# Hybrid decoder layer on one core: pieces of the third output column block placed between the seven products of the output projection

## The chip, the cores and the metric

The kernel runs on one core of one Trainium2 chip. The time is device microseconds (us) of one launch. Before the change it is 789.38 us, the median of 3 runs (789.31 to 791.33). A profiled execution of the same kernel took 789.26 us; its trace spans 787.5 us.

## The reference, cut to what matters

One layer on an input `x` of 256 tokens by 2048 channels, in float32. Two token mixers (gated DeltaNet and block attention) give `oa` and `ob`, each 256 x 1024. What follows them is the part that the change touches:

```
u_a = oa @ w_branch_a          # (256,1024) @ (1024,2048)
u_b = ob @ w_branch_b
merged = sigmoid(gate_a) * u_a + sigmoid(gate_b) * u_b
y = merged @ w_out             # (256,2048) @ (2048,2048)
out = x + rms_norm(y, post_norm_w)
```

## The kernel before, in words

**How a product is made.** TensorE works on float32 numbers that are split in two: `split` (L220 to L225) has ScalarE copy a raw piece of weights to a shorter format (`hi`, L223), and then VectorE subtract that from the raw piece (`lo`, L224). Three matmuls stand for one: hi by hi, hi by lo, lo by hi. One load of weights is 512 rows by 512 columns, 1 MB, issued by SyncE into one of three `raw` buffers. It is split in two **pieces**, each of 128 x 1024 numbers (two steps of 128 rows). `hi` and `lo` have three buffers each, so that piece n can be split only when TensorE has done with piece n-3. In the usual form (`proj_n`) a piece feeds two PSUM banks, one for each half of the tokens: 12 matmuls, a *double* piece. A piece that feeds one bank has 6 matmuls, a *single* piece.

**The order of the end of the kernel.** For each of four column blocks `c` of 512 channels the main loop makes `u_a` (`proj_n` with `wa`, four double pieces), multiplies the gate `ga` by it (L955), makes `u_b` (`wb`, four double pieces), multiplies `gb` (L958), and adds the two (L959). `merge(c)` then transposes the sum (`mt`, 2 x 4 matmuls of 128 x 128 on TensorE) and splits it into `mT` (ScalarE L929, VectorE L930).

The output projection has four column blocks as well. The top half of the first two column blocks (rows 0 to 1023 of `w_out`, columns 0 to 1023) is made by Strassen's scheme with **seven products** in place of eight: `product(...)` calls named yp1, yp5, yp6, yp2, yp7, yp3, yp4, each of two single pieces. They need sums of quarters of `mT` (four sums, made in `merge(1)` on VectorE, L935 to L938, and split by ScalarE L941 and VectorE L942) and differences of quarters of `w_out` (`tq`, six halves made by `differences()`, L915, and two more at L1003). The quarter `tq[0]` can be loaded, by GpSimd's queue (L903), only when the last sum is split, since it takes the sums' memory. Then come the bottom halves of column blocks 0 and 1 (double pieces, y0 and y1), then the whole of column block 2 (`proj_n` "y2", eight double pieces), then column block 3 (y3): its pieces are all split first (`keep`, L1058 and L1059, and two through `split`), and then multiplied for the first half of the tokens and for the second, each followed by its normalisation and output.

**What sets the order around the change.** Small jobs are Python generators in queues (`mq` for merges, `sq` for differences); `tick()` is called after every two-bank step of 128 rows (6 matmuls), in `product` after every one-bank step too, and lets a job go on when the units that it yielded have run out (half a unit per tick). So `yield 2` means four ticks. A list scheduler then lays out each engine's instructions; TensorE's order is the program's. ScalarE, VectorE and the DMA queues each work strictly through their own list. PSUM has eight banks: four for `acc` (here the four Strassen results c21, c11, c12, c22), four for `aux` (transposes).

Of the kernel before, what the change touches and what calls it, by code (L numbers as in the profile page):

```python
# [12 lines left out]
ALU = mybir.AluOpType  # L13
# [58 lines left out]
def hybrid_layer(  # L72
# [15 lines left out]
    nc = tc.nc  # L88
    B, S, D = x.shape
    NT = S // P  # L90
    KT = D // P
# [10 lines left out]
    wo = w_out.rearrange("o d f -> (o d) f")  # L102
# [16 lines left out]
    def acc_tile(name):  # L119
        return acc.tile([P, 512], F32, tag="acc", name=name)  # L120

    def aux_tile(name):
        return aux.tile([P, 512], F32, tag="aux", name=name)

    gq, vq, mq = Queue(), Queue(), Queue()
# [6 lines left out]
    def tick():  # L132
        after[0] -= 0.5
        for q in (gq, vq, mq, *aq, *extra):
            q.tick()
# [3 lines left out]
    def mm(*args, **kwargs):  # L139
        return pin(nc.tensor.matmul(*args, **kwargs))  # L140
# [79 lines left out]
    def split(raw, shape, name):  # L220
        hi = wspl.tile(shape, F32R, tag="hi", name=f"hi_{name}")
        lo = wspl.tile(shape, F32R, tag="lo", name=f"lo_{name}")
        nc.scalar.copy(hi, raw)  # L223
        nc.vector.tensor_tensor(lo, raw, hi.bitcast(F32), op=ALU.subtract)  # L224
        return hi, lo  # L225
# [9 lines left out]
    def turn(c):  # L235

        ks = range(CHUNKS[c], CHUNKS[c + 1])
        each = 1 if len(ks) == 2 else 2
        pts = []
        for i, k in enumerate(ks):  # L240
            if i % each == 0:
                pt = aux_tile(f"hTp_{k}")
            pts.append(pt[:, (i % each) * S : (i % each + 1) * S])
            for t in range(NT):
                tr(pts[-1][:, t * P : (t + 1) * P], xs[t][:, k * P : (k + 1) * P], ident)
        return [(k, pts[i]) for i, k in enumerate(ks)]
# [44 lines left out]
    pts = turn(0)  # L291
# [7 lines left out]
    for c in range(NCH):  # L299
        first_products("k", c, *sk_)  # L300
        if c == 0:
            pts = turn(1)
# [7 lines left out]
        if c + 2 < NCH:  # L310
            pts = turn(c + 2)
# [50 lines left out]
    def proj_n(w, col, stat, nk, name):  # L362

        pts = [acc_tile(f"a_{name}_{t}") for t in range(NT)]
        for kb in range(nk // 4):
            raw = wraw.tile([P, 4, 512], F32, tag="raw", name=f"raw_{name}_{kb}")
            nc.sync.dma_start(raw, w[kb * 512 : (kb + 1) * 512, col : col + 512].rearrange("(k p) c -> p k c", p=P))
            for u in range(2):
                hi, lo = split(raw[:, 2 * u : 2 * u + 2, :], [P, 2, 512], f"{name}_{kb}_{u}")
                for kk in range(2):  # L370
                    k = kb * 4 + u * 2 + kk
                    for t in range(NT):
                        sh = stat[:, k, t * P : (t + 1) * P]
                        sl = stat[:, k, S + t * P : S + (t + 1) * P]
                        mm(pts[t], sh, hi[:, kk, :], start=(k == 0), stop=False)
                        mm(pts[t], sh, lo[:, kk, :], start=False, stop=False)
                        mm(pts[t], sl, hi[:, kk, :], start=False, stop=(k == nk - 1))
                    tick()
        return pts
# [180 lines left out]
    def lazily(make):  # L560
        made = []

        def get():
            if not made:
                made.append(make())
            return made[0]

        return get
# [117 lines left out]
    ga = big.tile([P, D // 512, NT, 512], F32, tag="ga", name="ga")  # L686

    def free_tile(shape, dtype, tag, name):
        gq.drain()
        return big.tile(shape, dtype, tag=tag, name=name)  # L690

    gb_tile = lazily(lambda: free_tile([P, D // 512, NT, 512], F32, "g1", "gb"))
# [172 lines left out]
    for blk in ORDER:  # L865
        n, c = blk[:2].rstrip("0123456789"), int(blk[-1])
# [17 lines left out]
    mT = big.tile([P, KT, 2 * S], F32R, tag="hT", name="mT")  # L884
# [23 lines left out]
    load_quarter(2, 0, 0)  # L908

    def differences():  # L910
        yield 4
        for o, a, b in ((0, 0, 2), (1, 1, 0), (2, 1, 2)):
            for u in range(2):
                us = slice(2 * u, 2 * u + 2)
                nc.vector.tensor_tensor(tq[o][:, us], tq[a][:, us], tq[b][:, us], op=ALU.subtract)  # L915
                yield 2

    def merge(c):
        yield 1
        p3s = []  # L920
        for t in range(NT):
            pt = aux_tile(f"mt_{c}_{t}")
            for q in range(4):
                tr(pt[:, q * P : (q + 1) * P], ga[:, c, t, q * P : (q + 1) * P], ident)
            p3 = pt.rearrange("p (k n) -> p k n", n=P)
            p3s.append(p3)
            hi = mT[:, 4 * c : 4 * c + 4, t * P : (t + 1) * P]
            lo = mT[:, 4 * c : 4 * c + 4, S + t * P : S + (t + 1) * P]
            nc.scalar.copy(hi, p3)  # L929
            nc.vector.tensor_tensor(lo, p3, hi.bitcast(F32), op=ALU.subtract)  # L930
            if c == 0:
                nc.scalar.copy(sf[:, t], p3)
            yield 0.5
        if c == 1:
            nc.vector.tensor_tensor(sf[:, 2], p3s[1], sf[:, 1], op=ALU.add)  # L935
            nc.vector.tensor_tensor(sf[:, 3], sf[:, 2], sf[:, 0], op=ALU.subtract)
            nc.vector.tensor_tensor(sf[:, 1], sf[:, 0], sf[:, 1], op=ALU.subtract)
            nc.vector.tensor_tensor(sf[:, 0], p3s[0], sf[:, 3], op=ALU.subtract)  # L938
            yield 0.5
            for i, j in enumerate((2, 3, 1, 0)):  # L940
                nc.scalar.copy(SH[i], sf[:, j])  # L941
                nc.vector.tensor_tensor(SL[i], sf[:, j], SH[i].bitcast(F32), op=ALU.subtract)  # L942
                yield 0.5
            load_quarter(0, 0, 1)
            formed.append(True)
            sq.add(differences())
# [5 lines left out]
    for c in range(D // 512):  # L952
        pa = proj_n(wa, c * 512, oaT[0], H, f"ua{c}")
        for t in range(NT):
            nc.vector.tensor_tensor(ga[:, c, t, :], ga[:, c, t, :], pa[t], op=ALU.mult)  # L955
        pb = proj_n(wb, c * 512, ob_tile(), H, f"ub{c}")
        for t in range(NT):
            nc.vector.tensor_tensor(gb_tile()[:, c, t, :], gb_tile()[:, c, t, :], pb[t], op=ALU.mult)  # L958
            nc.vector.tensor_tensor(ga[:, c, t, :], ga[:, c, t, :], gb_tile()[:, c, t, :], op=ALU.add)  # L959
        mq.add(merge(c))  # L960


    sq.drain()
# [3 lines left out]
    def quarter(t, h):  # L967

        ks = slice(4 * h, 4 * h + 4)
        return mT[:, ks, t * P : (t + 1) * P], mT[:, ks, S + t * P : S + (t + 1) * P]  # L970

    def load(h, c):
        raw = wraw.tile([P, 4, 512], F32, tag="raw", name=f"raw_y{c}_{h}")
        nc.sync.dma_start(raw, wo[h * 512 : (h + 1) * 512, c * 512 : (c + 1) * 512].rearrange("(k p) c -> p k c", p=P))
        return raw

    def product(a, raw, banks, first, name):

        for u in range(2):
            hi, lo = split(raw[:, 2 * u : 2 * u + 2, :], [P, 2, 512], f"{name}_{u}")  # L980
            for kk in range(2):
                k = 2 * u + kk
                for (ah, al), pt, new in zip(a, banks, first):
                    mm(pt, ah[:, k], hi[:, kk, :], start=(new and k == 0), stop=False, skip_group_check=True)
                    mm(pt, ah[:, k], lo[:, kk, :], start=False, stop=False, skip_group_check=True)
                    mm(pt, al[:, k], hi[:, kk, :], start=False, stop=(k == 3), skip_group_check=True)
                tick()
# [2 lines left out]
    kept = big.tile([P, 3, 512], F32, tag="u1", name="kept")  # L990
    s1, s5, v = (kept[:, i] for i in range(3))
    s_ = list(zip(SH, SL))
    product([quarter(0, 0)], load(0, 0), [c21], [True], "yp1")
    product([s_[0]], tq[0], [c12], [True], "yp5")
    nc.scalar.copy(s1, c21)
    raw21 = load(1, 0)
    product([s_[1]], tq[1], [c21], [False], "yp6")
    nc.scalar.copy(s5, c12)
    product([quarter(0, 1)], raw21, [c11], [True], "yp2")
    nc.vector.tensor_tensor(c12, c21, s5, op=ALU.add)  # L1000
    for u in range(2):
        us = slice(2 * u, 2 * u + 2)
        nc.vector.tensor_tensor(tq[1][:, us], raw21[:, us], tq[1][:, us], op=ALU.subtract)  # L1003
    product([s_[2]], tq[2], [c21], [False], "yp7")
    product([s_[3]], load(1, 1), [c12], [False], "yp3")
    nc.vector.tensor_tensor(v, c21, s5, op=ALU.add)
    product([quarter(1, 1)], tq[1], [c21], [False], "yp4")

    postw = big.tile([P, D], F32, tag="z2", name="postw")
# [29 lines left out]
    for c, banks, late in ((0, (c11, c21), (c11, s1)), (1, (c12, c22), (c22, v))):  # L1039
# [2 lines left out]
        nc.vector.tensor_tensor(late[0], late[0], late[1], op=ALU.add)  # L1042
        for t in range(NT):
            weigh(c, t, banks[t])
    pts = proj_n(wo, 2 * 512, mT, KT, "y2")

    c, pts2 = 3, pts
    pts = [acc_tile(f"a_y{c}_{t}") for t in range(NT)]
    keep = [big.tile([P, 2, 2, 2, 512], F32R, tag=tg, name=f"keep_{tg}") for tg in ("g0", "ga", "u1")]
    parts = []  # L1050
# [51 lines left out]
```

## Time and profile before

| what | value |
|---|---|
| median of 3 runs | 789.38 us |
| profiled execution | 789.26 us |
| its span in the trace | 787.5 us |
| TensorE matmul busy | 98% of the span |
| VectorE busy | 67% |
| ScalarE busy | 52% |
| granted TensorE clock, mean | 0.998 |

The profile's page gives busy time by engine, 40 slices of the span, the chain of work that ended last, and the costliest groups of instructions. The trace behind it can be asked for one stretch: the busy time of each engine there, the instructions in order of time with what ended the idle time before them, and who waited for whom. Matmuls overlap each other by the profile's account (one of 128 x 512 is shown as 0.39 us long, while the next starts 0.23 us after it), so TensorE's starts say more than its ends.

### The profile page before, as it was taken

The page shows a single profiled execution, that of the slowest core. Times are in us where ns is not written, and L with a number is a line of the kernel's source. Part 1 is how long each engine was busy: PE and PEld are TensorE (multiplying, and loading weights), DVE is VectorE, ACT ScalarE, POOL GpSimd, SP SyncE. Part 2 cuts the span into 40 slices and gives each one's busy share as a digit, 9 for nine tenths or more (in the row PEclk, how much of TensorE's full clock was granted, in tenths as well). Part 3 has the DMA queues.
Part 4 walks back from the last instruction along what each step waited for, and adds up shares of the span by engine and source line. Part 5 has one row for each costly group of instructions (what it writes and reads, how often), then busy time and mean ns, then how long its engine had stood idle before and what let it go on. Part 6 is the DMA issues. An engine that isn't in the chain of part 4 may idle for free.

```text
span 787.5 us, 10153 instructions
## 1 busy us (share of the span) xinstructions
PE 771.8 (98%) x3869; PEld 647.6 (82%) x3869; DVE 531.5 (67%) x875; ACT 413.3 (52%) x624; POOL 26.2 (3%) x53
## 2 busy tenths in 40 slices
PE   8999999999999999999999999999999999999995
PEld 6878888888888888888888988888888887878884
DVE  5877885885868898864446556555545669797563
ACT  5776655554644545455365646454554444465451
POOL 3010000100100000020000000000000000000000
PEclk9999999999999999999999999999999999999999
DMA  9857656655596555686336375555466646667542
GB/s 269 263 148 221 202 165 177 210 162 164 175 277 226 188 191 189 209 221 207 107 108 199 124 219 178 187 163 164 158 214 213 203 172 213 195 228 260 174 159 107
DMA packets 95249, 149.78 MB, mean 190 GB/s; under 512 B 5152, under 2 KB 47184, under 8 KB 94560
## 3 DMA queue, kind: packets, MB, share of 16 engines
q1 hardware_dynamic: 92000, 136.46, 54.5%
q0 software_dynamic: 2624, 11.63, 5.1%
q10 hardware_dynamic: 576, 1.05, 0.4%
q8 instruction: 30, 0.49, 0.3%
q14 instruction: 19, 0.16, 0.1%
HBM read 145.95 MB, written 3.17 MB: 189 GB/s over the span
## 4 chain that ended last, share of the span: by engine, by line
PE 94%; DVE 2%; SPq 1%; ACT 1%; DMA 1%; issue 1%; DVEq 0%; ACTq 0%
PE a_ga L140 11%; PE a_gb L140 11%; PE a_y L140 10%; PE a_mk L140 6%; PE a_v L140 6%; PE a_mq L140 6%; PE a_zg L140 6%; PE a_zm L140 6%; PE a_ua L140 5%; PE a_q L140 5%; PE a_k L140 5%; PE a_ub L140 5%; PE a_mv L140 5%; PE sv L140 2%; PE s L140 1%; DMA x<-in_x_dram 1%
## 5 line engine op out<-in xcount | busy, mean ns | idle before, releaser
L140 PE MATMUL a_ga<-hi_ga,hT 128*128 128x512 f32 x256 | 82.2, 394 | 0.0
L140 PE MATMUL a_gb<-hi_gb,hT 128*128 128x512 f32 x256 | 82.1, 394 | 0.0
L224 DVE TENSOR_TENSOR lo_gb<-raw_gb,hi_gb 128x1024 fp32r<-128x1024 f32 x32 | 39.2, 1224 | 41.1 <-ACT hi_gb L223 41.1
L224 DVE TENSOR_TENSOR lo_ga<-raw_ga,hi_ga 128x1024 fp32r<-128x1024 f32 x32 | 39.0, 1223 | 30.2 <-ACT hi_ga L223 30.1
L223 ACT CAST hi_gb<-raw_gb 128x1024 fp32r<-128x1024 f32 x32 | 33.7, 1052 | 48.5 <-PE a_gb L140 34.5
L223 ACT CAST hi_ga<-raw_ga 128x1024 fp32r<-128x1024 f32 x32 | 33.5, 1051 | 47.1 <-PE a_ga L140 30.3
L140 PEld LDWEIGHTS a_ga<-hi_ga,hT 128*128 128x128 f32 x256 | 48.1, 188 | 11.0 <-issue 1.0
L140 PEld LDWEIGHTS a_gb<-hi_gb,hT 128*128 128x128 f32 x256 | 48.1, 188 | 10.0
L140 PE MATMUL a_ga<-lo_ga,hT 128*128 128x512 f32 x128 | 50.1, 391 | 0.0
L140 PE MATMUL a_gb<-lo_gb,hT 128*128 128x512 f32 x128 | 49.8, 389 | 0.0
L140 PE MATMUL a_k<-hT,hi_k 128*128 128x512 f32 x128 | 46.5, 404 | 0.1
L140 PE MATMUL a_mk<-hT,hi_mk 128*128 128x512 f32 x128 | 46.1, 401 | 0.0
L140 PE MATMUL a_mq<-hT,hi_mq 128*128 128x512 f32 x128 | 45.7, 400 | 0.0
L140 PE MATMUL a_q<-hT,hi_q 128*128 128x512 f32 x128 | 45.6, 397 | 0.0
L140 PE MATMUL a_v<-hT,hi_v 128*128 128x512 f32 x128 | 45.3, 397 | 0.0
L140 PE MATMUL a_y<-hi_y,mT 128*128 128x512 f32 x144 | 44.8, 389 | 0.0
L140 PE MATMUL a_ua<-hi_ua,oaT 128*128 128x512 f32 x128 | 41.8, 395 | 0.0
L140 PE MATMUL a_zg<-hi_zg,hT 128*128 128x512 f32 x128 | 40.6, 391 | 0.0
L140 PE MATMUL a_zm<-hi_zm,hT 128*128 128x512 f32 x128 | 40.5, 392 | 0.0
L140 PE MATMUL a_mv<-hi_mv,hT 128*128 128x512 f32 x128 | 40.5, 392 | 0.0
L140 PE MATMUL a_ub<-hi_ub,obT 128*128 128x512 f32 x128 | 40.1, 389 | 0.0
L140 PE MATMUL a_k<-hT,lo_k 128*128 128x256 f32 x128 | 36.2, 283 | 0.0
(333 smaller groups left out, 1906.1 us busy)
## 6 DMA issues: line engine op xcount, KB each, us to landing
raw_ga<-in_w_in_dram SPq DMA_DIRECT2D x16, 1024.0 KB, 5.3
raw_gb<-in_w_in_dram SPq DMA_DIRECT2D x16, 1024.0 KB, 5.1
raw_y<-in_w_out_dram SPq DMA_DIRECT2D x15, 1024.0 KB, 5.1
raw_mv<-in_w_in_dram SPq DMA_DIRECT2D x8, 1024.0 KB, 5.6
raw_zg<-in_w_in_dram SPq DMA_DIRECT2D x8, 1024.0 KB, 5.2
raw_v<-in_w_in_dram SPq DMA_DIRECT2D x8, 1024.0 KB, 5.5
raw_zm<-in_w_in_dram SPq DMA_DIRECT2D x8, 1024.0 KB, 5.1
raw_mq<-in_w_in_dram SPq DMA_DIRECT2D x8, 1024.0 KB, 5.7
```

What stands on the lines that cost most here:

```text
L140: return pin(nc.tensor.matmul(*args, **kwargs))
L223: nc.scalar.copy(hi, raw)
L224: nc.vector.tensor_tensor(lo, raw, hi.bitcast(F32), op=ALU.subtract)
```

## The change

- `merge(c)` now also holds the addition of the two gated branches (formerly L959 in the main loop) as its first step, and then waits half a unit before the transposes. For c = 0, 1, 2 that leaves the transposes where they were. `merge(3)` waits 5 units (ten ticks) first, so that its addition and transposes fall among the products.
- The four sums in `merge(1)` have a whole unit between their splits, in place of half a unit after them.
- `differences()` starts after 3 units in place of 4 and goes on every unit in place of every 2.
- Column block 2 is made by `third(h)`, a `product` of one load (512 rows, two double pieces), called four times: h = 0 after yp5, h = 1 after yp2, h = 2 after yp3, and h = 3 after the bottom halves of column blocks 0 and 1. It has two PSUM banks from `aux` in place of two from `acc`. The one `proj_n` call for column block 2 is gone. The number of matmuls, splits and loads is the same.

```diff
     def differences():
-        yield 4
+        yield 3
         for o, a, b in ((0, 0, 2), (1, 1, 0), (2, 1, 2)):
             for u in range(2):
                 us = slice(2 * u, 2 * u + 2)
                 nc.vector.tensor_tensor(tq[o][:, us], tq[a][:, us], tq[b][:, us], op=ALU.subtract)
-                yield 2
+                yield 1
 
-    def merge(c):
-        yield 1
+    def merge(c, wait=1):
+        yield wait
+        for t in range(NT):
+            nc.vector.tensor_tensor(ga[:, c, t, :], ga[:, c, t, :], gb_tile()[:, c, t, :], op=ALU.add)
+        yield 0.5
...
+            yield 0.5
             nc.vector.tensor_tensor(sf[:, 1], sf[:, 0], sf[:, 1], op=ALU.subtract)
             nc.vector.tensor_tensor(sf[:, 0], p3s[0], sf[:, 3], op=ALU.subtract)
-            yield 0.5
             for i, j in enumerate((2, 3, 1, 0)):
+                yield 1
                 nc.scalar.copy(SH[i], sf[:, j])
                 nc.vector.tensor_tensor(SL[i], sf[:, j], SH[i].bitcast(F32), op=ALU.subtract)
-                yield 0.5
...
-            nc.vector.tensor_tensor(ga[:, c, t, :], ga[:, c, t, :], gb_tile()[:, c, t, :], op=ALU.add)
-        mq.add(merge(c))
+        mq.add(merge(c, 0.5 if c < 3 else 5))
...
+    pts2 = [aux_tile(f"a_y2_{t}") for t in range(NT)]
+
+    def third(h):
+
+        product([quarter(0, h), quarter(1, h)], load(h, 2), pts2, [h == 0] * 2, f"y2_{h}")
+
     product([quarter(0, 0)], load(0, 0), [c21], [True], "yp1")
     product([s_[0]], tq[0], [c12], [True], "yp5")
     nc.scalar.copy(s1, c21)
+    third(0)
     raw21 = load(1, 0)
     product([s_[1]], tq[1], [c21], [False], "yp6")
     nc.scalar.copy(s5, c12)
     product([quarter(0, 1)], raw21, [c11], [True], "yp2")
     nc.vector.tensor_tensor(c12, c21, s5, op=ALU.add)
+    third(1)
...
     product([s_[3]], load(1, 1), [c12], [False], "yp3")
     nc.vector.tensor_tensor(v, c21, s5, op=ALU.add)
+    third(2)
     product([quarter(1, 1)], tq[1], [c21], [False], "yp4")
...
         for t in range(NT):
             weigh(c, t, banks[t])
-    pts = proj_n(wo, 2 * 512, mT, KT, "y2")
-
-    c, pts2 = 3, pts
+    third(3)
+
+    c = 3
     pts = [acc_tile(f"a_y{c}_{t}") for t in range(NT)]
```

## Prediction

> **What bounds the kernel now.** I read the page first. TensorE is busy for nearly the whole span, and it makes 94% of the chain that ended last.
>
> ```profile
> span 787.5 us, 10153 instructions
> PE 771.8 (98%) x3869; PEld 647.6 (82%) x3869; DVE 531.5 (67%) x875; ACT 413.3 (52%) x624; POOL 26.2 (3%) x53
> PE 94%; DVE 2%; SPq 1%; ACT 1%; DMA 1%; issue 1%; DVEq 0%; ACTq 0%
> ```
>
> The change leaves TensorE's work as it is, so it can win only what TensorE idles in the part that it reorders. The busy times by stretch, cut at the stages (columns: stretch, its length, then busy us and instructions by engine), show where that is: in the 13.0 us of `u_b` block 2 and in the 19.8 us of the seven products. In both VectorE is over 90% busy, against 77% and 58% in the stretches that follow them. From the products' end to TensorE's last matmul nothing is lost.
>
> ```profile
> core 0: us, PE busy (x) PEld busy (x) DVE busy (x) ACT busy (x) POOL busy (x), PEclk, DMA share, GB/s
> 655.49:668.50 13.01, 11.18 (x50) 8.94 (x49) 11.76 (x12) 4.21 (x4) 0.75 (x1) 1.00 0.70 242
> 668.50:691.22 22.72, 22.72 (x106) 18.76 (x104) 17.51 (x20) 9.51 (x10) 0.00 (x0) 1.00 0.57 185
> 691.22:711.05 19.83, 18.24 (x81) 13.99 (x80) 19.35 (x21) 14.57 (x16) 1.27 (x2) 1.00 0.70 258
> 711.05:757.00 45.95, 45.95 (x203) 37.85 (x202) 26.76 (x26) 21.14 (x27) 0.00 (x0) 1.00 0.64 215
> ```
>
> TensorE's waits (us, times, longest) name VectorE every time:
>
> ```profile
> PE a_ub L140 <- DVE lo_ub L224: 1.8, 1, 1.8
> PE a_y L140 <- DVE lo_yp L224: 1.4, 2, 1.0
> PE mt L143 <- DVE ga L959: 0.2, 1, 0.2
> ```
>
> Those add to 3.4 us. The timeline of TensorE gives more (start, length, and in brackets the idle time shown):
>
> ```profile
> 655.49 0.39 PE L140 MATMUL a_ub<-hi_ub,obT 128*128 128x512 f32 x1
> 657.71 0.50 PE L140 MATMUL a_ub<-lo_ub,obT 128*128 128x512 f32 x1 [1.83 <-DVE lo_ub L224]
> 658.04 0.62 PE L140 MATMUL a_ub<-hi_ub,obT 128*128 128x512 f32 x2
> ...
> 692.35 0.39 PE L140 MATMUL a_y<-hi_yp,mT 128*128 128x512 f32 x1
> 692.95 0.63 PE L143 MATMUL mt<-ident,ga 128*128 128x128 f32 x4 [0.21 <-DVE ga L959]
> ...
> 698.01 0.39 PE L140 MATMUL a_y<-hi_yp,sum_tv 128*128 128x512 f32 x1
> 698.30 0.50 PE L140 MATMUL a_y<-lo_yp,sum_tv 128*128 128x512 f32 x1
> 698.64 0.62 PE L140 MATMUL a_y<-hi_yp,sum_tv 128*128 128x512 f32 x2
> ...
> 700.93 0.39 PE L140 MATMUL a_y<-hi_yp,mT 128*128 128x512 f32 x1
> 701.71 0.50 PE L140 MATMUL a_y<-lo_yp,mT 128*128 128x512 f32 x1 [0.39 <-DVE lo_yp L224]
> 702.04 0.63 PE L140 MATMUL a_y<-hi_yp,mT 128*128 128x512 f32 x2
> ...
> 704.33 0.39 PE L140 MATMUL a_y<-hi_yp,sum_tw 128*128 128x512 f32 x1
> 705.71 0.50 PE L140 MATMUL a_y<-lo_yp,sum_tw 128*128 128x512 f32 x1 [0.99 <-DVE lo_yp L224]
> ...
> 711.28 0.50 PE L140 MATMUL a_y<-lo_yp,mT 128*128 128x512 f32 x1
> 711.61 0.64 PE L140 MATMUL a_y<-hi_yp,mT 128*128 128x512 f32 x2
> ```
>
> A matmul is shown 0.39 us long, but in an unbroken run they start 0.23 us apart; the chain of waits has one such run (below a group of transposes, which takes 0.44):
>
> ```profile
> 671.38 0.44 PE mt L143 x4
> ...
> 705.71 73.69 PE a_y L140 x323
> ```
>
> 73.69 / 323 = 0.228 us. So a stop costs the distance of two starts less 0.228: at 657.71 2.22 - 0.23 = 1.99, at 692.95 0.60 - 0.23 = 0.37, at 701.71 0.78 - 0.23 = 0.55, at 705.71 1.38 - 0.23 = 1.15. After a stop behind a `lo` the next start is 0.33 us away, 0.10 more (657.71 to 658.04, 701.71 to 702.04): 0.30 for these three. The small stop at 698.30 costs 0.29 - 0.23 and 0.11, the one at 711.28 0.10. In all **4.6 us**, the most that the change can win. The Trainium skill's page "Perfetto Trace Analysis" (Identifying the Most-Contended Engine) says that matmul busy time misjudges TensorE because matmuls are pipelined. Here it does: by idle time the ceiling would be 3.4 us, by starts it is 4.6.
>
> **Why VectorE is late.** A piece of weights costs ScalarE one `hi` and VectorE one `lo`; the other jobs stand in the same two lists.
>
> ```profile
> L223 ACT CAST hi_yp<-tq 128x1024 fp32r<-128x1024 f32 x8 | 8.3, 1052 | 3.9 <-PE a_y L140 2.2 <-PE a_ub L140 1.7
> L224 DVE TENSOR_TENSOR lo_yp<-tq,hi_yp 128x1024 fp32r<-128x1024 f32 x8 | 9.5, 1217 | 0.1
> L915 DVE TENSOR_TENSOR tq<-tq,tq 128x1024 f32<-128x1024 f32 x6 | 7.2, 1217 | 1.3 <-DMA tq<-in_w_out_dram 1.3
> ...
> 654.63 0.69 DVE L942 TENSOR_TENSOR sum_lo<-sums_f,sum_hi 128x512 fp32r<-128x512 f32 x1
> 655.24 1.28 DVE L955 TENSOR_TENSOR ga<-ga,a_ua 128x512 f32<-128x512 f32 x2
> 655.62 0.75 POOL L903 DMA_DIRECT2D tq<-in_w_out_dram  x1 [60.92 <-DVE sum_lo L942]
> 656.43 3.49 DVE L224 TENSOR_TENSOR lo_ub<-raw_ub,hi_ub 128x1024 fp32r<-128x1024 f32 x3
> ```
>
> Back to back a split takes VectorE (3.49 - 1.22) / 2 = 1.14 us, a 512-wide operation 1.28 - 0.68 = 0.60 us. A double piece lasts 12 x 0.228 = 2.73 us on TensorE, a single one 1.37: among the products a `lo` alone fills 83% of VectorE, and each further operation makes TensorE wait. The lead is set by the three buffers:
>
> ```profile
> 690.99 0.39 PE L140 MATMUL a_ub<-hi_ub,obT 128*128 128x512 f32 x1
> 691.42 1.06 ACT L223 CAST hi_yp<-tq 128x1024 fp32r<-128x1024 f32 x1 [1.67 <-PE a_ub L140]
> ```
>
> A `hi` starts 0.43 us after the last matmul start of the piece three before; with 1.09 (hi and handover) and 1.27 (1.22 and handover) `lo` is there 2.79 us after that start, and between two singles it is wanted at 2 x 0.228 + 2 x 1.37 = 3.20. A single piece thus has 0.4 us to spare; every double one between adds 1.37.
>
> **The change, part by part.** I walk the lists of the changed program, as the scheduler laid them, with these durations; lines are those of the kernel before.
>
> *Sums spread.* VectorE's list had the four sums' splits and `ga` ahead of the first `lo_ub`: that one began at 656.43 and TensorE got it at 657.71. Now `lo_ub` stands behind only one of the four splits (L942). The other three are 3 x 0.60 and the two `ga` 1.2, so it starts 3.0 us earlier, about 653.4, done at 654.6, wanted at 655.72. The rest follow in turns: `sum`, `ga` (its bank done at 655.7), `lo` at 656.3 for a piece wanted at 658.45, and so on with over 1 us each. **Gain 2.09** (1.99 + 0.10).
>
> *The quarter's load* waits for the last sum's split. That moves from 654.63 to about 659.2, so GpSimd issues at about 660.2.
>
> ```profile
> DMA to landing us min/median/max: 5.4/5.4/5.4
> ```
>
> It lands 5.4 later at 665.6. Its first reader now stands behind the `gb` and `ga` operations of block 2, at 668.5: 2.9 us to spare.
>
> *Differences.* Call U the start of `u_a` block 3 (668.50 before, 666.4 now). The six take 6 x 1.14 of VectorE as before, but the first two now come in one, at U+2.1 to U+4.4, ahead of `mT` and two `lo`. These are ready at U+6.2 and U+9.1, wanted at U+6.6 and U+9.3 (the two groups of transposes push these by 0.44 each): just in time. Next comes `ga` when its bank is done (U+12.0), a difference, and then `lo` of the second `u_b` piece: ready 12.0 + 1.2/2 + 1.14 + 1.27 = U+15.0, wanted at 11.8 + 2.73 + 0.23 = U+14.8. **Loss 0.25 + 0.10.**
>
> *Products with pieces between.* T is the first product's start. TensorE's list reads: yp1, yp5 (singles, T to T+5.5); two doubles with the transposes of `merge(3)` (to 11.8); yp6, yp2 (to 17.3); two doubles (22.7); yp7, yp3 (28.2); two doubles (33.6); yp4 (36.4). For each piece stands when `lo` is ready against when it is wanted:
> yp5: its first `hi` starts at 0.2, but VectorE has two `gb` and one `ga` from T-0.3 to T+1.5 (690.93 in the trace is 0.29 ahead of 691.22); then `lo`, ready at 2.8 for 3.0, and at 3.9 for 4.3.
> First double: ScalarE copies c21 (L995) when yp1 is done, at 2.9; `hi` from 3.4 to 4.5; `lo` from 4.5, ready at 5.8, wanted at 5.7. **Loss 0.1 + 0.1.** The other `ga` has its place just before it.
> yp6: 8.0 for 12.0 and 10.7 for 13.4, as the doubles give the lead. That leaves room on VectorE for the two L1003 and for `merge(3)`. yp2: 13.9 for 14.8 and 15.7 for 16.1.
> Next double, behind the addition L1000: 17.5 for 17.5. yp7: 2 us to spare. yp3: 25.2 for 25.7 and 26.6 for 27.0. Next double, behind L1006: 28.4 for 28.4. yp4: 2 us to spare.
> `mt` waits for nothing now: its addition is done by 4.4, its turn comes at 9.6. So of the 2.5 us of stops in this stretch 0.2 stay: **gain 2.3**.
>
> *SyncE's list* has the same 15 loads, four of them moved between. The block `raw21`, held for yp2 and L1003, keeps one of the three buffers until T+15.7, and the sixth load waits for that.
>
> *The tail.* y2's cover before y3 shrinks from eight pieces to two, but the three raw buffers had let y3's splits start only then anyway. The late addition of block 1 (L1042) and its two `yw` (L1023; 3 x 0.60) now fall in there. y3's pieces from the third on are ready 0.35 us or more ahead of need, as `weigh` is pinned in the same places: nothing.
>
> *Sum:* 2.09 + 2.3 - 0.35 = 4.04, less about 0 to 0.2 for the two places with nothing to spare: **4.1 to 3.9**. The profiled execution would go from 789.26 to 785.2; it lies 0.12 below the median, which is less than such a sum can tell.
>
> **Rivals.** (a) *VectorE's list runs late after all*: one more 0.60 operation of lag at each of the four tight places (the `lo` at U+6.2, the first double, those behind L1000 and L1006) costs 0.36 + 0.6 + 0.6 + 0.6 and three restarts of 0.1: 2.4 of the 4.1, time 787.6. For it: three of my margins are below 0.1 us; against it: VectorE recovers under each double piece.
> (b) *The quarter lands late* and a difference at the head of VectorE's list holds all splits behind it. It decides from a landing time of 5.4 + 2.9 = 8.3 us; at 11 the gain is 1.4, the time 787.9.
> (c) *It does not do what it says*: the waits put down to VectorE are something else's, and all come back: 789.3. Against it VectorE's unbroken rows around 656.
> (d) *Slower*: the sixth load, held by `raw21`. It is issued at T+15.8 and its `hi` must start by T+25.7. That allows 9.9 us to land. Each us beyond stops TensorE, so that from 14.0 the whole gain is gone; at 17 us the time is 792.3. Against it stand the landings of the 15 loads and, for size, of a 2 MB load (`hx`):
>
> ```profile
> DMA to landing us min/median/max: 5.0/5.1/6.6
> ...
> DMA to landing us min/median/max: 8.1/8.1/8.1
> ```
>
> The page "DMA: Bandwidth & Descriptors" of the Trainium skill (Queues, rings and completion order) says that an engine serves its queues by turns, which speaks against moving loads beside GpSimd's. By that a 1 MB load wholly beside `hx` would land in an estimated 5.1 + 8.1 = 13.2 us and cost 3.3. The trace only shows 6.6 at worst, and `hx` would be in by T+12.5, before that load is issued.
>
> **How the numbers follow.** The measurement tells about 0.3% (2.4 us). Forecast, a gain of 2.4 to 4.6 (784.6 to 787.0): 0.83. (a) at 787.0 to 788: 0.08. (b) 0.03, (c) 0.03, (d) 0.03. Only the forecast is faster by over 0.3%; (a) to (c) are the same, 0.14; slower 0.03. The range is the forecast's own, 784.5 to 787.0: its lower end is no stop left at all, with 0.1 for the spread of runs, its upper end reaches to (a).
>
> **What would show it.** The stop of 2 us at the first `lo_ub` of block 2 gone; among the products no stop over 0.3 us, VectorE below 85% busy there; a stop of some 0.3 us at the second `u_b` piece of block 3; 73 us of TensorE without a break to the end. Wrong it is if TensorE's list waits for a DMA, or if the stops come back at other `lo`.

## The result, and the profile after

The changed kernel takes **785.35 us**, the median of 4 runs (785.02 to 785.95). The kernel before, on the same chip, takes 790.36 us (789.31, 789.38, 791.33 and 791.34). The ratio is 0.9938, 95% interval 0.9919 to 0.9956: faster by 0.44 to 0.81%. The forecast was 785.2. The four times of before fall into two pairs, 2 us apart; what parts them came out in the last experiments below.

The head of the page of the changed kernel: the work is the same, the span 3.3 us shorter.

```profile
span 784.2 us, 10150 instructions
PE 771.6 (98%) x3869; PEld 647.9 (83%) x3869; DVE 531.9 (68%) x875; ACT 413.3 (53%) x624; POOL 26.2 (3%) x53
```

Asked for what TensorE waited for between 640 and 780 us, the view of the changed kernel has no row at all: the three rows of before, 3.4 us, are gone. The busy times by stretch, cut at the first matmul of `u_b` block 2, at `u_a` block 3, at the first product, and behind the last product (columns as before):

```profile
656.10:666.98 10.88, 10.88 (x50) 9.01 (x48) 8.16 (x10) 4.22 (x4) 0.75 (x1) 1.00 0.67 233
666.98:690.13 23.15, 23.05 (x106) 18.65 (x105) 21.04 (x23) 9.50 (x10) 0.00 (x0) 1.00 0.59 208
690.13:726.95 36.82, 36.82 (x165) 29.83 (x164) 29.65 (x30) 23.02 (x24) 1.27 (x2) 1.00 0.73 257
```

`u_b` block 2 went from 13.01 to 10.88 us. Block 3 grew from 22.72 to 23.15. The products now hold six double pieces too, so their 36.82 us has to be set against its own matmuls: 156 x 0.2275 + 2 x 0.44 (two groups of transposes) = 36.37, so 0.45 is lost there. The row of before that the prediction shows, to 711.05, ends in front of yp4 and so holds six of the seven products. With yp4 it reads:

```profile
691.22:713.94 22.72, 21.13 (x94) 16.17 (x92) 21.97 (x24) 16.67 (x18) 1.27 (x2) 1.00 0.74 273
```

By the same count 22.72 - (84 x 0.2275 + 2 x 0.44) = 2.7 us were lost before; the single stops add up to 2.5. VectorE's share fell from 21.97 / 22.72 = 97% to 29.65 / 36.82 = 81%.

The chain that ended last, in order of time (start, length, what), from the first matmul of `u_a` block 1 to TensorE's last:

```profile
644.44 2.72 PE a_ua L140 x12
...
656.26 10.88 PE a_ub L140 x48
...
679.63 1.22 DVE tq L915
680.85 1.15 DVE lo_ub L224
681.99 0.04 issue
682.04 8.25 PE a_ub L140 x35
...
702.32 73.76 PE a_y L140 x324
```

The chain of before begins that stretch with

```profile
643.84 2.72 PE a_ua L140 x12
```

and ends it with the row of 705.71 that the prediction shows. From 644.44 to 702.32 + 73.76 = 776.08 is 131.64 us; the same two points of before, 643.84 and 705.71 + 73.69 = 779.40, stand 135.56 us apart. The gain is **3.9 us**, inside the 4.1 to 3.9 that were summed. The two profiled executions differ by only 789.26 - 785.95 = 3.31 us, because the later one reached the first of these points 0.6 us later. That part precedes everything that was changed: the order of VectorE's list first differs at 653.2 us.

What is left of stops are these rows of TensorE's timeline (start, length). No idle time is noted behind them, so only the distances between the starts show them.

```profile
681.32 0.61 PE L140 MATMUL a_ub<-hi_ub,obT 128*128 128x512 f32 x2
682.04 0.50 PE L140 MATMUL a_ub<-lo_ub,obT 128*128 128x512 f32 x1
682.37 0.63 PE L140 MATMUL a_ub<-hi_ub,obT 128*128 128x512 f32 x2
...
695.62 0.39 PE L140 MATMUL a_y<-hi_y,mT 128*128 128x512 f32 x1
695.90 0.50 PE L140 MATMUL a_y<-lo_y,mT 128*128 128x512 f32 x1
696.24 0.62 PE L140 MATMUL a_y<-hi_y,mT 128*128 128x512 f32 x2
...
707.86 0.50 PE L140 MATMUL a_y<-lo_y,mT 128*128 128x512 f32 x1
708.19 0.64 PE L140 MATMUL a_y<-hi_y,mT 128*128 128x512 f32 x2
```

At 682.04 the stop costs 0.72 - 2 x 0.2275 = 0.26, and 0.10 for the restart (0.33 to the next start). At the first double piece of the products it costs 0.05 + 0.11, behind the addition that was L1000 0.10 (708.19), and behind the one that was L1006 0.11 (719.24, not shown). All four are places that the forecast named. VectorE's timeline shows the repair of block 2 and the new loss in block 3 from its side:

```profile
653.83 1.21 DVE L224 TENSOR_TENSOR lo_ub<-raw_ub,hi_ub 128x1024 fp32r<-128x1024 f32 x1
...
679.63 1.22 DVE L915 TENSOR_TENSOR tq<-tq,tq 128x1024 f32<-128x1024 f32 x1
680.77 1.22 DVE L224 TENSOR_TENSOR lo_ub<-raw_ub,hi_ub 128x1024 fp32r<-128x1024 f32 x1
```

The first `lo_ub` of block 2 now starts 2.27 us ahead of the block's first matmul (656.10); before, it started 0.94 behind it (656.43 against 655.49). The pair of rows below it is the loss: a difference stands ahead of the `lo` for which TensorE stops at 682.04.

### The profile page after: what moved, and what is told of

Read it like the earlier page. It is cut to its first block, busy times and chain, and to the rows that moved or that the text cites. A ratio compares the mean times of both kernels' runs of the same rounds, so it can differ in the third digit from the quotient of the medians.

```text
span 784.2 us, 10150 instructions
## 1 busy us (share of the span) xinstructions
PE 771.6 (98%) x3869; PEld 647.9 (83%) x3869; DVE 531.9 (68%) x875; ACT 413.3 (53%) x624; POOL 26.2 (3%) x53
## 4 chain that ended last, share of the span: by engine, by line
PE 94%; DVE 2%; SPq 1%; ACT 1%; DMA 1%; issue 0%; DVEq 0%; ACTq 0%
PE a_ga L140 11%; PE a_gb L140 11%; PE a_y L140 11%; PE a_mk L140 6%; PE a_v L140 6%; PE a_mq L140 6%; PE a_zg L140 6%; PE a_zm L140 6%; PE a_q L140 5%; PE a_k L140 5%; PE a_ub L140 5%; PE a_mv L140 5%; PE a_ua L140 5%; PE sv L140 2%; PE s L140 1%; DMA x<-in_x_dram 1%
```

## The experiments

The theory: TensorE stopped because VectorE's list put other work ahead of a `lo`, and each stop is worth its own length and some 0.1 us, so the parts of the change add up. Its rivals: the waits belong to something else; a late load decides; and, once two clusters of times were seen, that the clock takes a part of the gain.

### The waits alone, and the third column block alone

The change was cut in two. The first kernel has only the new waits of the sums and of `differences`, the same lines as in the change, and the addition in `merge`, the last merge early; column block 2 stays whole:

```diff
+    def merge(c, wait=1):
+        yield wait
...
-        mq.add(merge(c))
+        mq.add(merge(c, 0.5))
```

> Only the new waits of sums and differences; the third column block stays whole, and the last merge stays early. By the theory (VectorE's list runs late, in two places that have nothing to do with each other) the stop of 1.99 + 0.10 us at the first lo of u_b block 2 goes, the new stop of 0.26 + 0.10 at the second u_b piece of block 3 comes, and the 2.5 us of stops among the products stay as they were: 1.7 us faster than before, 2.2 us slower than the change. By the rival that the stretch as a whole is short of VectorE, so that what is won early is lost later, the stops among the products grow and the time is that of before.

Measured: 787.95 us (787.3 to 788.37), ratio 0.9968 [0.9956, 0.998]. TensorE's waits of this kernel:

```profile
PE a_y L140 <- DVE lo_yp L224: 1.3, 2, 0.9
PE mt L143 <- DVE ga L921: 0.2, 1, 0.2
```

The row of `lo_ub` is gone, the other two stand as before. By starts the stop of 2.0 is gone, 0.27 + 0.11 came at 682.25, and the products' stops are 0.37, 0.07, 0.55, 1.10 with their restarts of 0.1. Between the two points of the chain used above this kernel takes 133.80 us, 1.76 less than before; 1.7 was expected.

The second kernel has the rest: `third(h)` between the products and the last merge late, with the old waits of sums and differences:

```diff
+        mq.add(merge(c, 0.5 if c < 3 else 5))
...
+    third(0)
     raw21 = load(1, 0)
...
-    pts = proj_n(wo, 2 * 512, mT, KT, "y2")
+    third(3)
```

> Only the pieces of the third column block between the products and the late last merge; sums and differences keep their old waits. By the theory the stop of 2.1 us in u_b block 2 stays, none is seen in u_b block 3, and of 2.5 us among the products 0.3 to 0.4 stay: 2.1 to 2.3 us faster than before. By the rival that the spread sums and differences make the room for it, well under 1.5 us.

Measured: 787.48 us (787.06 to 790.4), ratio 0.9969 [0.9955, 0.9983]. Its waits are the mirror image:

```profile
PE a_ub L140 <- DVE lo_ub L224: 1.8, 1, 1.8
```

The stop of 1.98 stays, and the products keep 0.07 + 0.11, 0.10 and 0.10. Between the two points it takes 133.31 us, 2.25 less than before; 2.1 to 2.3 were expected. So each half removes its own stops and none of the other's, and 1.76 + 2.25 = 4.0 stands against 3.9 for both. That VectorE's order caused them is shown by this, and the rival that the waits belong to something else falls. By the ratios of times each half gains 2.5 us: in those the clock, of which more below, is mixed in.

### The last merge early

```diff
-        mq.add(merge(c, 0.5 if c < 3 else 5))
+        mq.add(merge(c, 0.5))
```

> The change with the last merge at its old place (a wait of half a unit in place of 5). By the theory only the stop of the first transposes behind the addition comes back, 0.37 us; lo of the pieces after it stays in time: 0.4 us slower than the change. By the rival that the late merge carries the gain, since the addition and the two mT subtractions fall on VectorE among singles, 1 us or more slower.

Measured: 786.02 us (785.54 to 786.24), ratio 0.9942 [0.9925, 0.9959]. One stop came back, 0.37 us at the transposes (691.82), and with it the one row of TensorE's waits, for `ga`, that the first kernel above still had. The late merge is worth 0.3 us between the two points of the chain and 0.37 by the stop alone. The two medians, 786.02 and 785.35, differ by a little more, which their spreads allow.

### One difference later

The change puts a difference ahead of a `lo` at 679.63. Here the pause ahead of that difference, the first of the last pair, is doubled, so that both fall behind a `lo`:

```diff
-                yield 1
+                yield 2 if (o, u) == (1, 1) else 1
```

> The change with the last pair of differences half a unit of four ticks later, so that in VectorE's list each stands behind the lo that it stood ahead of. By the theory the stop of 0.26 + 0.10 us at the second u_b piece of block 3 goes and nothing comes in its place: 0.36 us faster than the change, 785.0. By the rival that VectorE has no room left there, it comes back at a later piece.

Measured: 785.05 us (784.5 to 785.81), ratio 0.9939 [0.9924, 0.9953]. The stop of 0.26 + 0.10 is gone, and the chain of this kernel runs through the place on TensorE alone:

```profile
671.52 6.88 PE a_ua L140 x30
678.40 10.88 PE a_ub L140 x48
689.28 9.76 PE a_y L140 x42
```

That settles the cause of the one loss. By times alone it could not be told: 784.5 to 785.81 overlaps the change's 785.02 to 785.95. Between the two points of the chain it is the better by 0.4 us (131.21 for 131.64), with 0.4 us of stops left from block 1 on in place of 0.7.

### The quarter loaded twice

How much room has the load that the differences wait for? The change with a second, equal load of `tq[0]` right behind the first:

```diff
             load_quarter(0, 0, 1)
+            nc.gpsimd.dma_start(
+                tq[0], wo[0:512, 512:1024].rearrange("(k p) c -> p k c", p=P)
+            )
```

> The change with the last quarter of the output weights loaded twice, one load after the other, so that it is there some 11 us after the first issue in place of 5.4. By the theory VectorE's list stands still at the first difference from about 669 to 672 (2.9 us were to spare); the lo of the fourth u_a piece of block 3 behind it comes 1.4 us late, with 0.1 for the restart and perhaps 0.3 at the second u_b piece: a stop of about 1.5 us in u_a block 3, 1.4 to 1.9 us slower than the change. If the wait is covered anyway, 0; if each us of it counts, 3.

Measured: 795.04 us in one run, 9.1 more than the profiled execution of the change (785.95), where 1.4 to 1.9 were expected: the direction was right, the size was not. GpSimd's timeline of this kernel has the two loads (start, length, idle time before and what ended it):

```profile
660.85 0.75 POOL L903 DMA_DIRECT2D tq<-in_w_out_dram  x1 [65.72 <-DVE sum_lo L946]
667.50 0.75 POOL L948 DMA_DIRECT2D tq<-in_w_out_dram  x1 [5.90 <-DMA tq<-in_w_out_dram]
```

VectorE's has the first difference:

```profile
676.93 1.23 DVE L915 TENSOR_TENSOR tq<-tq,tq 128x1024 f32<-128x1024 f32 x1 [6.79 <-DMA tq<-in_w_out_dram]
```

TensorE's has the stop:

```profile
682.81 0.80 PE L140 MATMUL a_ua<-lo_ua,oaT 128*128 128x512 f32 x1 [6.51 <-DVE lo_ua L224]
683.41 1.05 PE L140 MATMUL a_ua<-hi_ua,oaT 128*128 128x512 f32 x2
684.26 0.63 PE L140 MATMUL a_ua<-lo_ua,oaT 128*128 128x512 f32 x1
```

And the landings of `tq` between 655 and 685 us, these two loads:

```profile
DMA to landing us min/median/max: 6.4/7.8/9.3
```

The first load landed in 6.4 us, the second in 9.3: from 668.2 to 670.9 the trace has SyncE's queue alone moving data (523 packets), and the second load's data only after that. So VectorE's list stood at its first difference for 6.79 us, every split behind it stood too, and TensorE stopped for 6.7 us. That is the mechanism of rival (b). But a stop of 6.7 us cost more than itself: behind it the matmuls start 0.43 us apart (683.41 to 684.26 for two), not 0.23, which loses another 2.9 us until 689. With the 0.36 of the change's own stop at 682.04, which is absent here, 6.7 + 2.9 - 0.4 makes up the 9.1. The busy times by stretch show the granted clock there (the eighth figure of a row, after five engines' busy times):

```profile
683.00:686.00 3.00, 3.00 (x8) 2.33 (x9) 2.03 (x2) 0.00 (x0) 0.00 (x0) 0.50 0.61 186
689.00:692.00 3.00, 3.00 (x15) 2.46 (x14) 3.00 (x4) 0.86 (x2) 0.00 (x0) 1.00 0.06 3
```

Half the clock and 8 matmuls seen in 3 us, against the full clock and 15. No expectation had reckoned with that, and it led to the last experiments.

### The two halves of L1003 on GpSimd

If VectorE is what runs late among the products, taking the two differences of yp4 (2 x 1.14 us) from it in the kernel before should shorten the stops.

```diff
-        nc.vector.tensor_tensor(tq[1][:, us], raw21[:, us], tq[1][:, us], op=ALU.subtract)
+        nc.gpsimd.tensor_tensor(tq[1][:, us], raw21[:, us], tq[1][:, us], op=ALU.subtract)
```

> The kernel before, with the two subtractions of L1003 on GpSimd in place of VectorE; nothing moved between the products. By the theory (VectorE is short of time among the singles, where 1.14 us more make TensorE wait) the stops of 0.55 and 1.15 us with their restarts of 0.1 go, those of 0.37 and 0.17 stay: 0.6 to 0.8 us of stops among the products in place of 2.5, 1.9 us faster. By the rival that only a longer lead between split and use helps (three hi and lo buffers are too few for single pieces), the stops stay at 2 us or more.

Measured: 792.92 us in one run. This failed: at yp2's first piece the stop grew from 0.55 to 1.62, and its second piece, which had none, now stops for 1.84. The stop of 1.15 at yp7's first piece, behind the second difference of L1003, shrank to 0.24, but TensorE now comes to that piece 3.0 us later, counted from the transposes, so this proves nothing. As a test of the theory the run is void, since it slowed what it meant to relieve. GpSimd's timeline at that place:

```profile
699.93 3.31 POOL L1003 TENSOR_TENSOR tq<-raw_y,tq 128x1024 f32<-128x1024 f32 x1 [3.92 <-DVE lo_yp L224]
703.20 3.36 POOL L1003 TENSOR_TENSOR tq<-raw_y,tq 128x1024 f32<-128x1024 f32 x1
```

VectorE's timeline, in two answers: the first split, and both splits as one row:

```profile
701.37 2.95 DVE L224 TENSOR_TENSOR lo_yp<-raw_y,hi_yp 128x1024 fp32r<-128x1024 f32 x1 [0.39 <-ACT hi_yp L223]
701.37 6.28 DVE L224 TENSOR_TENSOR lo_yp<-raw_y,hi_yp 128x1024 fp32r<-128x1024 f32 x2 [0.39 <-ACT hi_yp L223]
```

VectorE's two splits take 6.28 us, where two take 2.36 elsewhere. The first ends at 704.32, the second at 707.65: 1.08 and 1.09 us behind the ends of GpSimd's two operations (703.24 and 706.56). That is the time of a split alone, 1.14 us back to back: each split waited until GpSimd's whole operation was over. TensorE goes on at 704.37 and at 707.70. The page "SBUF — State Buffer" of the Trainium skill (SBUF: two separate sides) says that the two engines share a pair of ports under an exclusive lock, held for a whole instruction, by VectorE operations with two inputs in SBUF among others. This trace agrees with it.

### A longer stop, a shorter one, and the clock

The executions of the kernel before fall into two clusters by their mean granted clock. Of the 45 beside the experiments 21 have 0.997 or 0.998 and take 788.9 to 790.3 us (mean 789.71), 24 have 0.993 to 0.996 and take 790.4 to 792.4 (mean 791.26). The second kernel above, which keeps the stop of 2.0 us, shows two clusters too (787.1 to 787.6 and 788.8 to 790.4). The kernels without that stop show one. The trace of L1003 on GpSimd, the same as the kernel before up to that point, happened to catch it: behind its stop of 1.99 us matmuls start 0.43 us apart from 659.2 to 662.6. Its busy times by stretch (the clock is the eighth figure again):

```profile
655.70:659.11 3.41, 1.58 (x7) 1.21 (x7) 3.41 (x5) 1.04 (x1) 0.65 (x1) 1.00 0.50 167
659.11:662.52 3.41, 3.41 (x9) 2.64 (x9) 2.02 (x2) 0.88 (x1) 0.00 (x0) 0.50 1.00 371
```

The stop ends at 657.69, and the clock falls 1.4 us behind its end. The starts at half clock lose 1.55 us, and the means of the two clusters lie 1.54 apart. A further run of the kernel before, to catch it in its own trace, did not:

> The kernel before, unchanged, for a second profile: its times lie in two groups, 789.3 to 790.0 and 790.9 to 792.0, and those of the kernel with the 2 us stop left in (third pieces only) do so as well, while the kernels without that stop show one group. If the stop of 2.0 us lowers the granted clock in some executions, a profile of the slower group shows a clock under 1.00 right after the stop and the next matmuls 0.43 us apart for some 3 us, 1.5 to 2 us in all. By the rival that the two groups come from elsewhere (the start, loads), the clock after the stop is 1.00 in the slower group as well.

Measured: 789.1 us, a stop of 1.99 us, and a granted clock of 1.00 in every stretch behind it: a run of the lower cluster.

Next the stop was lengthened in the kernel before, by writing the third sum's split (0.60 us of VectorE) three more times ahead of the `lo`:

```diff
                 nc.vector.tensor_tensor(SL[i], sf[:, j], SH[i].bitcast(F32), op=ALU.subtract)
+                if i == 2:
+                    for _ in range(3):
+                        nc.vector.tensor_tensor(SL[i], sf[:, j], SH[i].bitcast(F32), op=ALU.subtract)
```

> The kernel before with the third sum's split written three times more than needed, all ahead of the first lo of u_b block 2: the stop there grows from 2.0 to 3.8 us. By work alone 1.8 us slower than the faster group of before (789.3), 791.1, with two groups as before. If a stop lowers the clock the more often the longer it is, nearly all runs fall in a slower group: 792.5 to 793.5, with a clock under 1.00 after the stop.

Measured: 794.03 us (793.76 to 794.53), ratio 1.0053 [1.0036, 1.0069], one cluster, clock 0.993 to 0.994 in every run. From TensorE's timeline:

```profile
659.94 0.50 PE L140 MATMUL a_ub<-lo_ub,obT 128*128 128x512 f32 x1 [3.63 <-DVE lo_ub L224]
```

and from its busy times by stretch:

```profile
661.00:664.00 3.00, 3.00 (x8) 2.32 (x8) 1.16 (x2) 0.00 (x0) 0.00 (x0) 0.50 0.82 322
```

By starts the stop is 3.79, which is 1.99 + 3 x 0.60: VectorE's list ahead of the `lo` sets it, to the tenth. Behind it the clock is half for 3.41 us (660.70 to 664.12), at a cost of some 1.6. The time is above the expected one because a new stop of 0.89 us came at the transposes (675.99), which waited for `ga`.

That shows a long stop lowering the clock, but not that the stop of 2.0 is what makes the clusters. For that the stop was put back into the **changed** kernel, which has one cluster, by writing the first `lo_ub` of block 2 a second time: half of it, the whole of it, and the whole with one of the sums (a subtraction of VectorE) written twice more.

```diff
         nc.vector.tensor_tensor(lo, raw, hi.bitcast(F32), op=ALU.subtract)
+        if name == "ub2_0_0":
+            nc.vector.tensor_tensor(lo, raw, hi.bitcast(F32), op=ALU.subtract)
```

> The changed kernel, with half of the first lo_ub of block 2 written a second time, so that TensorE stops there for about 1.2 us again (lo ready at about 657.5, wanted at 656.33). If the two groups of times of the kernel before come from a granted clock that falls after a long enough stop, 1.2 us is below the 2.0 of before and near the 1.1 us at which the earlier runs showed one group: one group at 785.35 + 1.3 = 786.6 us, mean clock 0.996 or more. Rival, that the groups come from something else in the kernel before (the sums' order, when the quarter is loaded): one group too, so this run alone does not tell them apart.

> The changed kernel, with the whole first lo_ub of block 2 written a second time: a stop of about 1.8 us there (lo ready at about 658.1), in a kernel that showed no second group. If the stop is what drops the clock, times in two groups come back: 785.35 + 1.9 = 787.2 us, and in part of the executions some 1.6 us more, 788.9, with a mean clock lower by 0.002 to 0.003. Rival, something else in the kernel before: one group at 787.2 us with the clock at 0.996 or more.

> The changed kernel as it is, beside the other two: one group around 785.35 us, mean clock 0.996 to 0.998; the rival has nothing against it.

> The kernel of e10_stop_long with one of the additions for the sums written twice more (one of the two delays the first lo_ub of block 2): a stop of 2.3 to 2.5 us there, where e10 had 1.85 and showed one group of times. If the length of the stop decides, with a bound between 1.85 and the 1.99 of the kernel before, the clock falls in more than half of the executions: those lie some 1.6 us above the others (788.6 and 790.2 us), mean clock 0.995 or lower. Rival, that something else in the kernel before makes its second group: one group at 788.6 us, clock 0.996 or more in all.

| kernel | stop by starts | times, us | clock |
|---|---|---|---|
| the change | none there | 785.89 (785.61 to 786.04), 5 runs | 0.996 to 0.998 |
| half written twice | 1.32 | 787.53 (786.84 to 788.12), 5 runs | 0.997 to 0.998 |
| whole written twice | 1.85 | 788.07 (787.81 to 788.41), 5 runs | 0.996 to 0.998 |
| whole twice, and two sums more | 2.36 | 789.64 (787.78 to 790.65), 12 runs | 2 runs at 0.997 and 0.998, 10 at 0.994 to 0.996 |

The half and the whole miss their expected times by 0.9 us. Of that 0.5 is the change itself, which took 785.89 beside them and not 785.35; the rest is a further stop of 0.43 and 0.51 at the transposes of block 3 (671.8 and 671.9), less the 0.36 at the second `u_b` piece of block 3, which they do not have. At 1.85 us the clock did not fall in any of five runs, against the expectation. At 2.36 it fell in most. In the last kernel the two runs with the higher clock are 787.78 and 788.22, the others 788.84 to 790.65. A mean of 0.996 alone does not tell (the change has it in some runs too); five of the ten have 0.994, which no kernel without the stop shows, and of the five with 0.996 one, a run of 790.49 us, has a trace. TensorE's timeline in it:

```profile
656.57 0.39 PE L140 MATMUL a_ub<-hi_ub,obT 128*128 128x512 f32 x1
659.16 0.73 PE L140 MATMUL a_ub<-lo_ub,obT 128*128 128x512 f32 x1 [2.21 <-DVE lo_ub L226]
659.69 1.05 PE L140 MATMUL a_ub<-hi_ub,obT 128*128 128x512 f32 x2
660.54 0.63 PE L140 MATMUL a_ub<-lo_ub,obT 128*128 128x512 f32 x1
...
662.91 0.39 PE L140 MATMUL a_ub<-lo_ub,obT 128*128 128x512 f32 x1
```

Between 659.69 and 662.68 the starts are 0.43 us apart; from 659.16 to 662.91 they lose 1.7 us. So the same drop comes up in the kernel that was free of it, once the stop is long enough: the stop makes the second cluster, and the rival (something else in the kernel before) falls.

Why only some executions of one kernel fall can be read from the kept traces as well. In all fourteen the granted clock changes only at moments that lie whole multiples of 3.413 us apart (190 of them, for example, from the clock's first rise to its fall in the trace above). Such moments divide each execution into windows, which lie differently over its stop each time. For the long stop of each trace, taken from one usual distance (0.2275 us) behind the last start to the next start, this is the most of it that falls into one window:

| kernel of the trace | stop, us | most of it in one window | clock behind that window |
|---|---|---|---|
| half written twice | 1.32 | 1.32 | 1.00 |
| third column block alone | 1.99 | 1.34 | 1.00 |
| the kernel before, second profile | 1.99 | 1.38 | 1.00 |
| the kernel before, first profile | 1.99 | 1.69 | 1.00 |
| whole written twice | 1.85 | 1.01 | 1.00 |
| L1003 on GpSimd | 1.99 | 1.99 | 0.50 |
| whole twice, and two sums more | 2.36 | 2.36 | 0.50 |
| the quarter loaded twice | 6.67 | 2.37, then 3.41 | 0.50 |
| a longer stop | 3.79 | 2.65 | 0.50 |

The busy times of the window that holds the 1.69 (of the first profile); the clock is 1.00 in the next window too:

```profile
654.00:657.41 3.41, 1.88 (x9) 1.22 (x7) 3.27 (x5) 1.64 (x3) 0.75 (x1) 1.00 0.10 14
```

Four stops of the same 1.99 us fare differently by where they lie: three are cut in two by the end of a window, and the one that lies wholly in a window halves the clock. So the bound lies between 1.69 and 1.99 us of a stop within a window of 3.41, that is between 50% and 58% of it. If the windows lie at random, such a bound makes a stop lower the clock in an estimated share of (3.41 + stop - 2 x bound) / 3.41 of the executions: 42 to 59% at 1.99 us, 53 to 70% at 2.36. Measured were 24 of 45 and 10 of 12. At 1.85 us a bound of 1.69 would give 55%, and a bound over 1.85 none, so the five runs without a fall speak for the upper end. Only one of these five has a trace, with at most 1.01 us in a window, so this stays open.

## Why the prediction was right, point by point

- **Sums spread**, gain 2.09: `u_b` block 2 became 2.13 us shorter. Right, and shown alone by the kernel with the waits only.
- **The quarter's load**, issued at 660.2, landing in 5.4, 2.9 us to spare. In the timelines of GpSimd and VectorE in the changed kernel, which stand 0.61 us later by then (656.10 for 655.49):

```profile
661.02 0.75 POOL L903 DMA_DIRECT2D tq<-in_w_out_dram  x1 [65.71 <-DVE sum_lo L946]
669.09 2.35 DVE L915 TENSOR_TENSOR tq<-tq,tq 128x1024 f32<-128x1024 f32 x2
```

  and the answer for `tq`:

```profile
DMA to landing us min/median/max: 6.4/6.4/6.4
```

  Issue at 661.02 (660.4 in the trace of before), landing at 667.4, first reader at 669.09: 1.7 us to spare. Two things ate the 1.2: the landing was 1.0 longer than in the one row that the forecast had, and the issue 0.2 later. It did not matter, but the margin was thinner than said, and the second load of the experiment landed in 9.3: rival (b) deserved more than 0.03.
- **Differences**, loss 0.25 + 0.10 at the second `u_b` piece of block 3: measured 0.26 + 0.10, at that piece. The kernel with one later difference shows that it was this.
- **Products with pieces between**, gain 2.3 with 0.2 left at the first double piece and 0 to 0.2 at the two places with nothing to spare: measured 0.16 at the first double piece, 0.10 and 0.11 at the two places. The groups of transposes wait for nothing there, as said, and the early merge puts the 0.37 back.
- **SyncE's list**: the sixth load was expected to be issued at T+15.8, with 9.9 us to land; it was issued at 706.09, which is T+15.96, and landed in 4.9. Rival (d) named the right danger for the wrong load. The fifth, issued at 697.01 beside the 2 MB `hx` (issued at 694.89), took 9.8 us, the largest landing of `raw_y` from 685 us on:

```profile
DMA to landing us min/median/max: 4.9/5.0/9.8
```

  Its first reader came at 713.44, 6.7 us after the landing. `hx` itself took 9.7 us in place of 8.1. The estimate of 13.2 us by the Trainium skill's page "DMA: Bandwidth & Descriptors" (Queues, rings and completion order) was for a load that lies wholly beside `hx`; this one overlapped with it for 7.6 us. 13.2 us is also the time by which both loads would be in: by equal turns the 1 MB alone would be in after twice 5.1, an estimated 10.2 us, and cost 0.3. The queues' packets from the fifth load's issue to 700.9 show no turns at all:

```profile
q0 software_dynamic: 177, 1.45, 93.5%
q1 hardware_dynamic: 1, 0.00, 0.1%
```

  GpSimd's queue (q0) had the engines to itself while the fifth load, on SyncE's (q1), waited; its data moved from then on. So here the load that came first was served first, and the measurement decides against the turns for this stretch. In the kernel with the quarter loaded twice both queues did move data side by side (131 and 123 packets from 664 to 666 us). What decides between the two is not shown.
- **The tail**, nothing: 73.76 us without a break from 702.32 to the end.

The sum, 4.1 to 3.9 (its terms as written give 4.04 to 3.84), stands against 3.9 in the traces. Two readings of it were off without moving the sum: its row of "the seven products" leaves out yp4, and "from the products' end nothing is lost" leaves out the 0.10 at 711.28, in yp4, which its ceiling of 4.6 does count. What the prediction did not have is the clock. It set the profiled execution against the median "0.12 below", took the spread of the three runs (789.31 to 791.33) for noise, and so missed that about half of the executions of the kernel before pay some 1.6 us for the stop beyond its length. Between the 21 runs of before with the higher clock and the nine of the change the gain is 789.71 - 785.64 = 4.1; between the medians of one comparison it is 790.36 - 785.35 = 5.0, more than the ceiling of 4.6 that the prediction set. That 785.35 lies so near the forecast of 785.2 is in part luck: the forecast counted from a profiled execution that had kept its clock, and the profiled execution of the change took 785.95.

## What to carry to other kernels

Lay the due time of every operand of the busiest engine beside its ready time, piece by piece and in the order of the helper engine's list: where spare time is below one small operation, a stop of a few tenths will stand, and its place can be named beforehand. Count stops by the distance of matmul starts, since the views note no idle time for those left here. When a kernel's times fall in two clusters, look for the longest stop of TensorE and at the granted clock behind it before calling the spread noise.

## What the runs showed of the hardware that was not expected

- **A stop of 2 us can halve TensorE's clock**, in the executions in which it falls into one window. The clock changes only at the ends of windows of 3.413 us. It fell behind every window that held 1.99 us or more of a stop (four traces) and stayed up behind those with up to 1.69 (five). So the fall is a matter of chance from run to run: the mean clock was lower in 24 of 45 executions with a stop of 1.99 us, in 10 of 12 (five of them beyond doubt) with 2.36, in 4 of 4 with 3.79 and in none of 5 with 1.85. The half clock was granted for 3.41 us in three traces, which cost 1.6 to 1.7 us, and for 10.24 around the stop of 6.7, which cost 2.9 behind it. The Trainium skill's page "TensorE: Matmul & The Clock Gate" (Part 1: The HAM clock gate) says that the gate falls to half after at least one idle window of about 3.4 us, and that the window runs freely. The halving, the length of the window and its running freely are borne out. That the whole window must be idle is not: a window with 1.99 us of idle was enough.
- **GpSimd and VectorE excluded each other** on float32 subtractions of two tiles in SBUF, in the one run that tried it: a 1.14-us split of VectorE took 2.95 and 3.3 us beside a GpSimd operation shown as 3.3 us long, and ended 1.1 us behind it.
- **Landing times of 1 MB** were 5.0 us alone, 6.4 and 9.3 us for GpSimd's load beside SyncE's, and 9.8 us for SyncE's beside GpSimd's 2 MB; in the two longest the later load moved next to no data until the earlier one was nearly through.
